# The start addresses of matmul operands in a decoder layer on one core, laid out anew

## The chip, the cores and the metric

The kernel runs on one core of one Trainium2 chip. The metric is the device time of one execution in microseconds. Three runs of the kernel before took 2182.17, 2182.19 and 2182.4 us, median 2182.19.

## The reference

One decoder layer in float32 for 512 tokens of width 2048. What is computed:

```python
hn = rms_norm(x, norm_mix_pre)
q, k, v, gate_b, gate_c, hc = split(hn @ w_in)          # 2048 -> 6 x 1024
a = rms_norm(diff_attention(q, k, v, lam, rel_bias), subln_gain) * (1 - lambda_init)
c = rms_norm(gate_b * short_conv(gate_c * hc, conv_w), conv_norm_gain)
x = x + rms_norm(concat(a, c) @ w_out, norm_mix_post)
hn = rms_norm(x, norm_ffn_pre)
f = (silu(hn @ w_gate) * (hn @ w_up)) @ w_down          # 2048 -> 5632 -> 2048
x = x + rms_norm(f, norm_ffn_post)
```

`diff_attention` has 8 heads; each is the difference of two causal softmaxes (64 wide) with a relative-position bias, times v (128 wide).

## The kernel before

Every large product is done in three passes of a faster 32-bit matmul type (fp32r). An operand is split into a high part, rounded to that type by ScalarE (`split`, L99), and a low part, the rest, by VectorE (L100). `mm3` (L121 to L124) then issues three matmuls for one block of 128 rows of the contraction: high x high (L122), high x low (L123), low x high (L124). In its argument list the first pair, `lhi, llo`, is the stationary operand (128x128, loaded as weights), the second, `rhi, rlo`, the moving one, streamed in 256 or 512 columns. In the profile PE is the matmul, PEld the load of its weights; while one matmul streams, the weights of the next are loaded.

The stages, in order of time:

1. v, first half of its columns, while x is normalised and transposed into `act_hi` and `act_lo` (4 token tiles x 16 blocks x 128, so 32 KB per partition each). Moving: chunks of w_in; stationary: act.
2. v, second half; then 20 column projections (`job_cols`: q, k, h, c, b, four times). Here act moves, 512 columns at a time, and w_in is stationary. Attention for two heads at a time is stepped between them as side work; so are its small matmuls, with tiles of their own (q, k, klo, v, whi, wlo).
3. The output projection (`job_out`, `out_last`). Moving: w_out; stationary: act, which now holds attention and convolution.
4. The norm before the feed-forward part, its transposes (`to_x`) and the sums of quadrants of x that a Strassen scheme needs (`t1` to `t4`).
5. Gate and up (`gate_up`). Each 256 columns of w_gate or w_up are a quartet of blocks, 44 in all, worked in 7 products instead of 8 (`product`). A product is 8 x `mm3` = 24 matmuls of 256 moving columns; the moving operand comes from act or from one of the pairs x0/x1, x2/x3, x4/x5 (`moving`), and `w` is stationary, both parts in one ring tile (high part first, low part 4 KB behind). Product 6 moves x0/x1, product 7 x2/x3, product 4 x4/x5, the others act. Products run in the order 1, 2, 5, 7, 6, 3, 4, but the first four matmuls of product 5 stand ahead of product 2, which waits for ScalarE to copy product 1 out of the bank that it shares.
6. Down (`job_down`, `down_last`): 44 blocks of the hidden activations in 5 groups of 4, 12, 12, 12 and 4. Moving: w_down, 512 columns; stationary: the hidden activations, in group 0 in spare and m3, in groups 1 and 3 in act, in groups 2 and 4 in x0 to x5.

Weights come in chunks of 8 KB per partition into `raw`, are split by ScalarE and VectorE, and the parts go round a ring of four tiles of 8 KB (`ring_tile`): a chunk of w_in, w_out or w_down takes two of them (so the pairs 0, 1 and 2, 3 alternate), a `w` of gate and up takes one. In stage 1 and in the last parts of stages 3 and 6 some chunks go to tiles of another pool (`part` in stage 1, `two_parts` into x tiles later).

Where an operand begins in its partition is set by the pools. In the kernel before, `offset_tile` (L75) asks for a tile of 8 KB + 128 bytes (32 KB + 128 for act) that starts at a multiple of 128 bytes, and uses it from 32 bytes on; a `w` in the ring is used from 96 bytes on (L798, `ring_tile(16, P, ..., 24)`, offsets being in words of 4 bytes). Later tiles lie behind earlier ones, so successive tiles move on by 128 bytes or more. The feed-forward tiles x0 to x5, spare and m3 are made the same way in `place`. Within a tile every block that a matmul reads begins a multiple of 512 bytes from the start of the operand.

Of the kernel before, what the change touches and what calls it, by code (L numbers as in the profile page):

```python
# [12 lines left out]
F32R = mybir.dt.float32r  # L13
# [5 lines left out]
P = 128  # L19
D = 2048  # L20
S = 512
NT = S // P
KC = D // P
# [30 lines left out]
def trunk(ctx: ExitStack, tc: tile.TileContext, a, out):  # L54
    nc = tc.nc
    w_in, w_out, w_gate, w_up, w_down = (a[n][0] for n in ("w_in", "w_out", "w_gate", "w_up", "w_down"))
    x = a["x"][0]
# [8 lines left out]
    def mm_bank(name):  # L66
        return ps.tile([P, 512], F32, tag="mm", name=name)
# [4 lines left out]

    high = ctx.enter_context(tc.tile_pool(name="high", bufs=1, side="right"))

    def offset_tile(pool, words, n, m, tag, name, offset=8, **kw):  # L75

        t = pool.tile([P, words + 32], F32R, tag=tag, name=name, align_bytes=128, **kw)
        return t[:, offset : offset + n * m].rearrange("p (n m) -> p n m", m=m)

    act_hi, act_lo = (  # L80
        offset_tile(high, NT * KC * P, NT * KC, P, n, n).rearrange("p (t k) n -> p t k n", k=KC)
        for n in ("act_hi", "act_lo")
    )
    ring = [0]

    def ring_tile(n, m, name, offset=8):

        i = ring[0] = (ring[0] + 1) % 4
        return offset_tile(high, 2048, n, m, f"ring{i}", name, offset)

    ident = const.tile([P, P], F32, name="ident")
    make_identity(nc, ident)
# [5 lines left out]
    def split(hi, lo, src):  # L98
        nc.scalar.copy(hi, src)  # L99
        nc.vector.tensor_tensor(out=lo, in0=src, in1=hi.bitcast(F32), op=ALU.subtract)  # L100
# [20 lines left out]
    def mm3(o, lhi, llo, rhi, rlo, start, stop):  # L121
        nc.tensor.matmul(o, lhsT=lhi, rhs=rhi, start=start, stop=False)  # L122
        nc.tensor.matmul(o, lhsT=lhi, rhs=rlo, start=False, stop=False)  # L123
        nc.tensor.matmul(o, lhsT=llo, rhs=rhi, start=False, stop=stop)  # L124
# [14 lines left out]
    def scale_rows(xn, xt, r, gB, k4):  # L139
        cs = slice(k4 * 512, (k4 + 1) * 512)  # L140
        nc.vector.scalar_tensor_tensor(
            out=xn[:, cs], in0=xt[:, cs], scalar=r, in1=gB[:, cs], op0=ALU.mult, op1=ALU.mult
        )
# [34 lines left out]
    with start as sp:  # L178
        xts, vch, early = [], [], []
        gB = sp.tile([P, D], F32, tag="gain", name="g_norm_mix_pre")  # L180

        def load_x(t):
            xt = sp.tile([P, D], F32, tag="x", bufs=NT, name=f"x_{t}")
            for c in range(2 if t == 0 else 1):
                cs = slice(c * 1024, (c + 1) * 1024) if t == 0 else slice(0, D)
                nc.sync.dma_start(xt[:, cs], x[t * P : (t + 1) * P, cs])
            xts.append(xt)

        def load_gain(c):
            cs = slice(c * 1024, (c + 1) * 1024)  # L190
            nc.sync.dma_start(gB[:, cs], a["norm_mix_pre"][0:1, cs].broadcast_to([P, 1024]))

        def part(n):
            def parts(name):
                return tuple(offset_tile(sp, 2048, 4, 512, f"{x_}{n}", f"{x_}_{name}") for x_ in ("hi", "lo"))

            return parts

        def v_spec(cg, q4):
            c0 = 2 * A + cg * 512  # L200
            return w_in[q4 * 512 : (q4 + 1) * 512, c0 : c0 + 512], 4, 512, f"v{cg}_{q4}"

        vb = [mm_bank(f"pv_0_{t}") for t in range(NT)]

        def v_part(t, q4):
            for k in range(4):
                kc = 4 * q4 + k
                mm3(vb[t], act_hi[:, t, kc, :], act_lo[:, t, kc, :], vch[q4][0][:, k, :], vch[q4][1][:, k, :], kc == 0, kc == KC - 1)

        def first_norm(t):  # L210
            xn = sp.tile([P, D], F32, tag="xn", bufs=2, name=f"xn_{t}")
            ss = small.tile([P, 2], F32, tag="ss2", name=f"ss_{t}")
            for c in range(2):
                cs = slice(c * 1024, (c + 1) * 1024)
                nc.scalar.activation(xn[:, cs], xts[t][:, cs], AF.Square, accum_out=ss[:, c : c + 1])
            nc.vector.tensor_add(ss[:, 0:1], ss[:, 0:1], ss[:, 1:2])
            r = rsqrt_mean(ss[:, 0:1], 1, D, EPS, f"pre{t}")
            for k4 in range(4):
                scale_rows(xn, xts[t], r, gB, k4)
                to_act(t, xn, k4, f"pre{t}")  # L220

        def v_load(q4):
            vch.append(load_chunk(*v_spec(0, q4), part(q4) if q4 >= 2 else None))

        def bias_rows():

            oh = sp.tile([NB, VL], F32, tag="oh", name="oh")
            nc.sync.dma_start(oh, a["bucket_rows"])
            rb = sp.tile([NB, NH], F32, tag="rb", name="rb")
            nc.sync.dma_start(rb, a["rel_bias"])  # L230
            vec = sp.tile([NH, VL], F32, tag="vec", name="vec")
            for i in range(2):
                b = aux_bank(f"pvec_{i}")
                nc.tensor.matmul(b[:NH, : VL // 2], lhsT=rb, rhs=oh[:, i * (VL // 2) : (i + 1) * (VL // 2)], start=True, stop=True)
                nc.vector.tensor_copy(vec[:, i * (VL // 2) : (i + 1) * (VL // 2)], b[:NH, : VL // 2])
            d1 = dram.tile([NH, VL], F32, name="d1")
            nc.scalar.dma_start(d1, vec)
            d2 = dram.tile([P, NH, VL], F32, name="d2")
            nc.scalar.dma_start(d2, bass.AP(d1.tensor, d1.offset, [[0, P], [VL, NH], [1, VL]]))
            return d2  # L240

        load_x(0)
        load_gain(0)
        load_gain(1)
        first_norm(0)
        v_load(0)
        v_part(0, 0)
        v_load(1)
        load_x(1)
        v_part(0, 1)  # L250
        first_norm(1)
        v_load(2)
        v_load(3)
        load_x(2)
        load_x(3)
        for q4 in range(2):
            v_part(1, q4)
        for q4 in range(2, 4):
            for t in range(2):
                v_part(t, q4)  # L260
        for t in range(2, NT):
            first_norm(t)
            if t == 2:
                d2 = bias_rows()
            for q4 in range(4):
                v_part(t, q4)
                if t == NT - 1 and q4 < 2:
                    early.append(load_chunk(*v_spec(1, q4)))
# [294 lines left out]
    late = {}  # L563
# [5 lines left out]
    def place(tag, dtype=F32, shape=(P, D)):  # L569
        count = late["count"] = late.get("count", 0) + 1  # L570
        name = f"{tag}_{count}"
        if tag[0] == "x" or tag in ("spare", "m3"):
            t = late["fp"].tile([P, D + 32], dtype, tag=tag, bufs=1, name=name, align_bytes=128)
            t = t[:, 8 : 8 + D]
            return t.rearrange("p (n m) -> p n m", m=shape[-1]) if len(shape) == 3 else t
        return late["fp"].tile(list(shape), dtype, tag=tag, bufs=1, name=name)

    def open_ffn(_):
# [24 lines left out]
        return late["mix"][t][:, half * 1024 : (half + 1) * 1024]  # L603

    def act_half(t, half):
        return tuple(x_[:, t, 8 * half : 8 * half + 8, :].rearrange("p k n -> p (k n)") for x_ in (act_hi, act_lo))

    def t_half(n, tau):
        if n not in late:
# [19 lines left out]
    def to_x(t, k4):  # L629

        xn = late["mix"][t][:, k4 * 512 : (k4 + 1) * 512]
        b = aux_bank(f"px_{t}_{k4}")
        for i in range(4):
            nc.tensor.transpose(b[:, i * P : (i + 1) * P], xn[:, i * P : (i + 1) * P], ident)
        nc.scalar.copy(xn, b)
        if t < 2 or k4 >= 2:
            sl = slice(4 * k4, 4 * k4 + 4)
            split(*(x_[:, t, sl, :].rearrange("p k n -> p (k n)") for x_ in (act_hi, act_lo)), b)

    def residual_in(t):  # L640
        late["x", t] = place(f"x{4 + t % 2}")
# [146 lines left out]
    def prepare(n):  # L788

        q, i = order[n]  # L790
        if i in (1, 2) and 0 < q < HEAD:
            src = heads_raw[q][:, 8 * (i - 1) : 8 * i, :]
        else:
            (p11, p21), (p12, p22) = ((r[:, :, :P], r[:, :, P:]) for r in raws[q])
            src = {1: p11, 2: p12, 3: p12, 4: p22, 5: tmp.get("s1"), 6: p21, 7: p21}[i]
            if i in (3, 6):
                combine(q, {3: 4, 6: 2}[i])
        w = ring_tile(16, P, f"w_{q}_{i}", 24).rearrange("p (a k) m -> p a k m", a=2)  # L798
        split(w[:, 0], w[:, 1], src)
        operands[n] = w  # L800

    def moving(i, part, k):
        x_ = (act_hi, act_lo)[part]
        if i in (1, 2):
            return x_[:, 0:2, 8 * (i - 1) + k, :]
        if i in (3, 5):
            return x_[:, 2:4, (8 if i == 3 else 0) + k, :]
        return late[{6: 2, 7: 3, 4: 4}[i]][part].rearrange("p (t k n) -> p t k n", t=2, n=P)[:, :, k, :]
# [215 lines left out]
```

## Time and profile before

| | |
|---|---|
| median of three runs | 2182.19 us |
| the profiled execution | 2182.11 us |
| its span, first to last instruction | 2180.3 us |
| granted TensorE clock, mean | 0.997 |
| PE, PEld busy | 99%, 88% |
| DVE, ACT busy | 60%, 37% |
| chain that ended last | PE 96%, DVE 3%, DMA 1% |
| HBM traffic | 120 GB/s over the span |
| first matmul of gate and up, last one | 792.6 us, 1684.5 us |

A matmul's recorded duration (280 ns at 256 columns, about 390 at 512) overlaps the next matmul's, since matmuls are pipelined: a busy PE says little. What counts is how far apart two matmuls begin, which the timeline gives to 0.01 us, and how many begin in a stretch, which the windows give. PEld is a row of its own: 99% of it in gate and up means that the loads follow each other without a gap.

### The profile page before, as it was taken

What the parts mean: (1) busy time and instruction counts of PE and PEld (TensorE: products, weight loads), DVE (VectorE), ACT (ScalarE), POOL (GpSimd) and SP (SyncE); (2) the same over time, 40 slices, a digit from 0 to 9 for tenths busy, and PEclk for the clock granted to TensorE, in tenths of its full rate; (3) what the DMA queues carried; (4) which work ended last, traced back from release to release, by engine and by line L of the source; (5) the groups of instructions that cost most, each with busy time, mean ns of one, the idle gap of its engine ahead of it and who ended that gap; (6) DMA issues with size and microseconds to landing.
All of it is one profiled execution on the core that took longest, in us unless ns stands there. A gap on an engine that the chain in (4) does not pass through costs nothing.

```text
span 2180.3 us, 30431 instructions
## 1 busy us (share of the span) xinstructions
PE 2149.8 (99%) x13118; PEld 1914.0 (88%) x13118; DVE 1312.7 (60%) x1635; ACT 809.0 (37%) x1065; POOL 30.1 (1%) x51
## 2 busy tenths in 40 slices
PE   7999999999999998999999999999999999999998
PEld 6788888888888888999999999999999888888886
DVE  5226355453642489888888887887887532432336
ACT  4234243433532364444444444444444321211122
POOL 0000000000000000000000000000000000000000
PEclk9999999999999999999999999999999999999999
DMA  7322223222243353343343333333423632423233
GB/s 242 110 97 87 97 86 99 88 85 90 78 177 113 136 174 117 116 136 98 116 136 121 103 126 126 116 108 126 136 95 122 219 135 97 155 97 116 96 115 117
DMA packets 197831, 261.74 MB, mean 120 GB/s; under 512 B 9368, under 2 KB 146584, under 8 KB 195264
## 3 DMA queue, kind: packets, MB, share of 16 engines
q1 hardware_dynamic: 196384, 255.05, 34.7%
q10 hardware_dynamic: 1312, 4.74, 0.7%
q8 instruction: 103, 1.69, 0.3%
q14 instruction: 32, 0.26, 0.0%
HBM read 240.88 MB, written 21.52 MB: 120 GB/s over the span
## 4 chain that ended last, share of the span: by engine, by line
PE 96%; DVE 3%; DMA 1%; issue 0%; ACT 0%; POOL 0%; SPq 0%; DVEq 0%; POOLq 0%; ACTq 0%
PE pd L124 9%; PE pd L123 9%; PE pd L122 9%; PE pa L122 4%; PE pc L124 4%; PE pc L123 4%; PE pc L122 4%; PE pb L122 4%; PE pb L124 4%; PE pb L123 4%; PE pa L124 3%; PE pa L123 3%; PE po L124 3%; PE po L122 3%; PE po L123 3%; PE pv L123 1%
## 5 line engine op out<-in xcount | busy, mean ns | idle before, releaser
L100 DVE TENSOR_TENSOR lo_d<-raw_d,hi_d 128x2048 fp32r<-128x2048 f32 x42 | 96.2, 2291 | 188.1 <-ACT hi_d L99 188.1
L122 PE MATMUL pa<-act_hi,w 128*128 128x256 f32 x704 | 201.7, 286 | 0.7 <-ACT w L99 0.7
L124 PE MATMUL pa<-act_hi,w 128*128 128x256 f32 x704 | 198.3, 282 | 0.3 <-DVE w L100 0.3
L123 PE MATMUL pa<-act_lo,w 128*128 128x256 f32 x704 | 196.9, 280 | 0.0
L99 ACT CAST w<-raw_q 128x1024 fp32r<-128x1024 f32 x130 | 136.5, 1051 | 139.4 <-PE pc L124 39.4
L99 ACT CAST hi_d<-raw_d 128x2048 fp32r<-128x2048 f32 x42 | 80.3, 1913 | 283.1 <-PE pd L124 266.1
L100 DVE TENSOR_TENSOR w<-raw_q,w 128x1024 fp32r<-128x1024 f32 x130 | 156.7, 1221 | 13.7 <-ACT w L99 13.7
L124 PE MATMUL pd<-hi_d,act_lo 128*128 128x512 f32 x384 | 151.4, 394 | 0.0
L122 PE MATMUL pd<-hi_d,act_hi 128*128 128x512 f32 x384 | 150.9, 393 | 0.0
L123 PE MATMUL pd<-lo_d,act_hi 128*128 128x512 f32 x384 | 150.3, 392 | 0.0
L122 PEld LDWEIGHTS pa<-act_hi,w 128*128 128x128 f32 x704 | 132.2, 188 | 8.9 <-ACT m L833 7.9
L124 PEld LDWEIGHTS pa<-act_hi,w 128*128 128x128 f32 x704 | 132.5, 188 | 0.5 <-DVE w L100 0.5
L123 PEld LDWEIGHTS pa<-act_lo,w 128*128 128x128 f32 x704 | 132.7, 188 | 0.0
L124 PE MATMUL pb<-act_hi,w 128*128 128x256 f32 x352 | 98.8, 281 | 3.0 <-DVE w L100 3.0
L122 PE MATMUL pd<-x,w 128*128 128x256 f32 x352 | 99.0, 281 | 1.7 <-ACT w L99 1.7
L124 PE MATMUL pd<-x,w 128*128 128x256 f32 x352 | 99.2, 282 | 1.3 <-DVE w L100 1.3
L124 PE MATMUL pc<-act_hi,w 128*128 128x256 f32 x352 | 98.6, 280 | 0.3 <-DVE w L100 0.3
L123 PE MATMUL pd<-x,w 128*128 128x256 f32 x352 | 98.8, 281 | 0.0
L122 PE MATMUL pb<-x,w 128*128 128x256 f32 x352 | 98.7, 281 | 0.0
L123 PE MATMUL pc<-act_lo,w 128*128 128x256 f32 x352 | 98.7, 280 | 0.0
L123 PE MATMUL pb<-x,w 128*128 128x256 f32 x352 | 98.7, 280 | 0.0
L124 PE MATMUL pb<-x,w 128*128 128x256 f32 x352 | 98.7, 280 | 0.0
(283 smaller groups left out, 6140.3 us busy)
## 6 DMA issues: line engine op xcount, KB each, us to landing
raw_q<-in_w_gate SPq DMA_DIRECT2D x44, 1024.0 KB, 5.1
raw_d<-in_w_down SPq DMA_DIRECT2D x44, 1024.0 KB, 5.0
post<-in_w_up SPq DMA_DIRECT2D x22, 1024.0 KB, 5.1
pre<-in_w_up SPq DMA_DIRECT2D x22, 1024.0 KB, 5.1
raw_o<-in_w_out SPq DMA_DIRECT2D x16, 1024.0 KB, 5.0
hd<-m SPq DMA_DIRECT2D x20, 512.0 KB, 2.8
raw_h<-hd SPq DMA_DIRECT2D x10, 1024.0 KB, 5.3
raw_v<-in_w_in SPq DMA_DIRECT2D x8, 1024.0 KB, 5.8
```

The lines of the kernel that those rows point to most:

```text
L99: nc.scalar.copy(hi, src)
L100: nc.vector.tensor_tensor(out=lo, in0=src, in1=hi.bitcast(F32), op=ALU.subtract)
L122: nc.tensor.matmul(o, lhsT=lhi, rhs=rhi, start=start, stop=False)
L123: nc.tensor.matmul(o, lhsT=lhi, rhs=rlo, start=False, stop=False)
L124: nc.tensor.matmul(o, lhsT=llo, rhs=rhi, start=False, stop=stop)
```

## The change

The padded tiles go. `acts` is one tile that holds act high and low for the projections at words 16 and 8336, and for gate and up at words 0 and 8320, which is 64 bytes lower; these `ffn_hi` and `ffn_lo` overlay the others, and gate and up, with the steps that fill them, now use them. Ring tiles, the start stage's tiles, x0 to x5, spare and m3 are plain tiles of 8 KB. The number, the order, the sizes and the waits of all instructions on all engines are the same in both built programs.

The start of each operand within 512 bytes, from the tile addresses in the two built programs:

| operand | before | after |
|---|---|---|
| act_hi, act_lo in stages 1 to 3, and in down | 288, 416 | 480, 480 |
| act in gate and up (after: ffn_hi, ffn_lo) | 288, 416 | 416, 416 |
| ring tiles 0, 1, 2, 3 with w_in, w_out, w_down | 160, 416, 160, 288 | 480, all four |
| ring tiles 0, 1, 2, 3 with `w` of gate and up | 224, 480, 224, 352 | 480, all four |
| x0, x1, x2, x3, x4, x5 | 160, 416, 160, 416, 32, 288 | 416, all six |
| spare, m3 | 32, 32 | 416, 416 |
| stage 1's own hi and lo tiles (two chunks) | 32, 160 and 416, 160 | 416, all four |
| attention: q, k, klo, v | 416 | 416 |
| attention: whi, wlo, token tiles 0 and 2; 1 and 3 | 416; 480 | 416; 480 |

Whole addresses, in bytes of the partition: before, act_hi begins at 129824, act_lo at 162720, the ring tiles at 195744, 204192, 212640 and 220960; after, act_hi at 130528, act_lo at 163808, the ring at 196576, 204768, 212960 and 221152, 8192 apart.

```diff
-    def offset_tile(pool, words, n, m, tag, name, offset=8, **kw):
-
-        t = pool.tile([P, words + 32], F32R, tag=tag, name=name, align_bytes=128, **kw)
-        return t[:, offset : offset + n * m].rearrange("p (n m) -> p n m", m=m)
-
-    act_hi, act_lo = (
-        offset_tile(high, NT * KC * P, NT * KC, P, n, n).rearrange("p (t k) n -> p t k n", k=KC)
-        for n in ("act_hi", "act_lo")
-    )
+    acts = high.tile([P, 2 * NT * KC * P + 144], F32R, name="acts")
+    act_hi, act_lo, ffn_hi, ffn_lo = (
+        acts[:, o : o + NT * KC * P].rearrange("p (t k n) -> p t k n", k=KC, n=P)
+        for o in (16, 144 + NT * KC * P, 0, 128 + NT * KC * P)
+    )
...
-    def ring_tile(n, m, name, offset=8):
+    def ring_tile(n, m, name):
...
-        return offset_tile(high, 2048, n, m, f"ring{i}", name, offset)
+        return high.tile([P, n, m], F32R, tag=f"ring{i}", name=name)
...
-                return tuple(offset_tile(sp, 2048, 4, 512, f"{x_}{n}", f"{x_}_{name}") for x_ in ("hi", "lo"))
+                return (
+                    sp.tile([P, 4, 512], F32R, tag=f"hi{n}", name=f"hi_{name}"),
+                    sp.tile([P, 4, 512], F32R, tag=f"lo{n}", name=f"lo_{name}"),
+                )
...
-        if tag[0] == "x" or tag in ("spare", "m3"):
-            t = late["fp"].tile([P, D + 32], dtype, tag=tag, bufs=1, name=name, align_bytes=128)
-            t = t[:, 8 : 8 + D]
-            return t.rearrange("p (n m) -> p n m", m=shape[-1]) if len(shape) == 3 else t
         return late["fp"].tile(list(shape), dtype, tag=tag, bufs=1, name=name)
...
-        return tuple(x_[:, t, 8 * half : 8 * half + 8, :].rearrange("p k n -> p (k n)") for x_ in (act_hi, act_lo))
+        return tuple(x_[:, t, 8 * half : 8 * half + 8, :].rearrange("p k n -> p (k n)") for x_ in (ffn_hi, ffn_lo))
...
-            split(*(x_[:, t, sl, :].rearrange("p k n -> p (k n)") for x_ in (act_hi, act_lo)), b)
+            split(*(x_[:, t, sl, :].rearrange("p k n -> p (k n)") for x_ in (ffn_hi, ffn_lo)), b)
...
-        w = ring_tile(16, P, f"w_{q}_{i}", 24).rearrange("p (a k) m -> p a k m", a=2)
+        w = ring_tile(16, P, f"w_{q}_{i}").rearrange("p (a k) m -> p a k m", a=2)
...
-        x_ = (act_hi, act_lo)[part]
+        x_ = (ffn_hi, ffn_lo)[part]
```

## The prediction

> **What bounds the kernel now.** I read the page's busy times and its chain first, then windows of the long stages, then the timeline of single matmuls.
>
> ```profile
> span 2180.3 us, 30431 instructions
> PE 2149.8 (99%) x13118; PEld 1914.0 (88%) x13118; DVE 1312.7 (60%) x1635; ACT 809.0 (37%) x1065; POOL 30.1 (1%) x51
> ...
> PE 96%; DVE 3%; DMA 1%; issue 0%; ACT 0%; POOL 0%; SPq 0%; DVEq 0%; POOLq 0%; ACTq 0%
> ...
> 1000.00:1200.00 200.00, 200.00 (x1682) 198.03 (x1681) 163.18 (x175) 86.96 (x95) 0.00 (x0) 1.00 0.36 119
> 1200.00:1400.00 200.00, 200.00 (x1683) 198.03 (x1682) 163.11 (x175) 87.06 (x96) 0.00 (x0) 1.00 0.36 119
> 1400.00:1600.00 200.00, 200.00 (x1682) 198.03 (x1681) 163.12 (x175) 86.95 (x96) 0.00 (x0) 1.00 0.36 119
> 1728.88:1861.99 133.11, 133.11 (x577) 108.11 (x576) 44.85 (x31) 29.01 (x16) 0.00 (x0) 1.00 0.38 134
> ```
>
> The last four rows are windows; their columns are PE, PEld, DVE, ACT, POOL busy, then clock, DMA share and GB/s. The chain of work is TensorE for 96%, at a granted clock of 1.00, so the time is a count of matmuls times their spacing. I call the time from one matmul's start to the next one's start its pitch. In gate and up 5047 matmuls of 256 columns take 600 us: 118.9 ns each, and there the weight loads (PEld) are busy 99% of the time. In the second down group 577 matmuls of 512 columns take 133.1 us: 230.7 ns each, with PEld busy 81%. So a matmul of 256 columns waits for its weights as much as for its data, and one of 512 columns has room for the load. DVE (82% in gate and up) and DMA (36%) are below their limits.
>
> No instruction, size or wait differs in the changed kernel; only addresses do. The question is what a pitch owes to addresses. While one matmul streams its moving operand, the weights of the next one are loaded. I call D the start of that moving operand minus the start of those weights, in bytes, modulo 512. The table of tile starts ahead of this gives D for every pair. Four chains of 512 columns, each by its first and last start (48, 48, 48 and 4 matmuls):
>
> ```profile
> 1795.44 0.39 PE L122 MATMUL pd<-hi_d,act_hi 128*128 128x512 f32 x1
> ...
> 1806.40 0.40 PE L124 MATMUL pd<-hi_d,act_lo 128*128 128x512 f32 x1
> 1806.64 0.39 PE L122 MATMUL pd<-hi_d,act_hi 128*128 128x512 f32 x1
> ...
> 1817.40 0.39 PE L124 MATMUL pd<-hi_d,act_lo 128*128 128x512 f32 x1
> ...
> 1906.03 0.39 PE L122 MATMUL pd<-hi_d,x 128*128 128x512 f32 x1
> ...
> 1916.68 0.40 PE L124 MATMUL pd<-hi_d,x 128*128 128x512 f32 x1
> ...
> 183.73 0.40 PE L415 MATMUL pss<-k,q 128*128 128x512 f32 x1
> ...
> 184.42 0.39 PE L416 MATMUL pss<-klo,q 128*128 128x512 f32 x1
> ```
>
> The first chain (ring tiles 0 and 1 against act; D 384, 0, 384 over the three matmuls of `mm3`) has a pitch of 10.96/47 = 233.2 ns; the second, same code on ring tiles 2 and 3 (D 384, 384, 384), 10.76/47 = 228.9. The third (ring tiles 0 and 1 against x2 and x3: D 0, 0, 0) has 10.65/47 = 226.6. The fourth, attention scores, has D 0 and all its tiles alike modulo 512, as the change makes nearly every operand; its three pitches are 230 on average, right after other phases. So address alone is worth 6.6 ns of 233, and D = 0 is the lowest.
>
> Now 256 columns: product 6 of quartets 20, 21 and 22 (24 matmuls each), then attention values of an even and an odd head (8 each), and a shorter one (4):
>
> ```profile
> 1216.03 0.28 PE L122 MATMUL pd<-x,w 128*128 128x256 f32 x1
> ...
> 1218.64 0.28 PE L124 MATMUL pd<-x,w 128*128 128x256 f32 x1
> ...
> 1235.95 0.28 PE L122 MATMUL pd<-x,w 128*128 128x256 f32 x1
> ...
> 1238.66 0.28 PE L124 MATMUL pd<-x,w 128*128 128x256 f32 x1
> ...
> 1255.96 0.28 PE L122 MATMUL pd<-x,w 128*128 128x256 f32 x1
> ...
> 1258.67 0.28 PE L124 MATMUL pd<-x,w 128*128 128x256 f32 x1
> ...
> 198.41 0.28 PE L416 MATMUL pss<-klo,q 128*128 128x256 f32 x1
> 198.53 0.28 PE L458 MATMUL pa<-v,whi 128*128 128x256 f32 x1
> ...
> 199.36 0.28 PE L458 MATMUL pa<-v,wlo 128*128 128x256 f32 x1
> 225.88 0.39 PE L124 MATMUL pc_b<-act_hi,lo_b 128*128 128x512 f32 x1
> 226.11 0.28 PE L458 MATMUL pa<-v,whi 128*128 128x256 f32 x1
> ...
> 226.90 0.28 PE L458 MATMUL pa<-v,wlo 128*128 128x256 f32 x1
> 184.66 0.28 PE L458 MATMUL pa<-v,whi 128*128 128x256 f32 x1
> ...
> 185.01 0.28 PE L458 MATMUL pa<-v,wlo 128*128 128x256 f32 x1
> ```
>
> Quartet 20 (w in ring tile 0; D 448, 192, 448) runs at 2.61/23 = 113.5 ns. Quartet 21 (ring tile 3; D 320, 64, 320) runs at 2.71/23 = 117.8, and quartet 22, whose ring tile 2 gives the same D as ring tile 0, at 117.8 too. The two heads have D 448 throughout, the value that the change gives all of gate and up: the even head runs at 0.83/7 = 118.6, the odd one at 0.79/7 = 112.9. So there are two steady pitches, about 117.7 and 113.4, and the address does not settle alone which one a chain takes. What came before does: the odd head follows a matmul of 512 columns, with its weights long loaded; the even head follows 256-column scores at the upper pitch, and stays there. The 118.9 of gate and up says that nearly all its products are at the upper one.
>
> **The change part by part.** The sum is made against the profiled execution, 2182.11 us (span 2180.3 and 1.8 around it), which is the median of 2182.19 within 0.1.
>
> *Gate and up* (44 quartets x 7 products x 24 = 7392 matmuls). Moving operands begin 64 bytes below the weights, so D is 448 everywhere, and it no longer jumps by 128 or 256 bytes between high and low parts or between products. Part of the 118.9 is a stall in each quartet:
>
> ```profile
> 987.52 0.28 PE L122 MATMUL pb<-act_hi,w 128*128 128x256 f32 x1
> 987.79 0.38 PE L122 MATMUL pa<-act_hi,w 128*128 128x256 f32 x1
> 988.01 0.28 PE L123 MATMUL pa<-act_lo,w 128*128 128x256 f32 x1
> ...
> L122 PEld LDWEIGHTS pa<-act_hi,w 128*128 128x128 f32 x704 | 132.2, 188 | 8.9 <-ACT m L833 7.9
> ```
>
> Pitches of 270 and 220 instead of twice 117.7: 255 ns per 168 matmuls, 1.5 ns each, so the undisturbed pitch is 117.4. It is not removed. At the lower pitch the gain is 4.0 x 7392 = 29.6 us. Against it: after a stall the pitch has to settle again (the short chain above: three pitches in 0.35 us, 12 ns over 3 x 113.4), and the four matmuls that cover ACT's copy get 4 ns shorter each: 28 ns x 44 = 1.2 us. Net 28.4. Bounds: nothing (the upper pitch stays), and 113.4 without either loss, 29.6. I take the lower pitch because gate and up is entered from 512-column matmuls of the output projection, as the odd head is, every stall gives the load the same head start, and nothing afterwards shifts D. DVE then works 16.3 us of a quartet of 19.3 us (84%), so its splits still keep ahead.
>
> *512 columns, D = 0.* This holds for 1152 matmuls of down (groups 1 and 3, against act), about 670 of the output projection, 290 of v, all 1920 of the column projections and 96 of the last down group. Down alternates 233.2 and 228.9, mean 231.1; the output projection and v use the same ring pairs against act, so I price them alike. The column projections go by this chain (q and k of the first pair, 192 matmuls):
>
> ```profile
> 115.56 0.39 PE L122 MATMUL pc_q<-act_hi,hi_q 128*128 128x512 f32 x1
> ...
> 159.29 0.39 PE L124 MATMUL pc_k<-act_hi,lo_k 128*128 128x512 f32 x1
> ```
>
> 43.73/191 = 229.0. At 226.6: down, output, v and the rest 2208 x 4.5 = 9.9 us; columns 1920 x 2.4 = 4.6, less some 50 interruptions by attention that each cost three or four pitches of 230 instead of 226.6 (0.7 us). Together 13.8. Bounds: nothing, if they stay at the 230 of the scores (columns 2 us longer, the rest 2 us shorter), and 14.5.
>
> *512 columns, D = 64 or 448.* In 864 matmuls of down (groups 0, 2 and half of the last) the weights lie in x, spare or m3, 64 bytes below the ring; in some 190 of v and output it is the other way round. No chain of 512 columns here has either. Bounds from the chains above, 226.6 and 233.2 around today's mean of about 229.5: a gain of 3 us or a loss of 4. I take 0, the middle.
>
> *ACT, DVE, DMA.* Same work into other addresses. TensorE's 99% covers them; only the head and the norm between the output projection and gate would show a change, and an instruction there would have to get much slower to matter.
>
> Sum: 28.4 + 13.8 = 42.2 us; 2182.1 - 42.2 = 2140 us.
>
> [...]
>
> **The rivals.**
> *Gate and up keep the upper pitch*, as quartet 22 does with the same D as quartet 20: for it speaks that 117.7 is the common state, against it that D then jumped at each product and now does not. 2182 - 13.8 = 2168. Or they take it by turns, ring tile by ring tile: half of the 28.4, 2154.
> *Nothing moves*: the sum over an `mm3` triple is fixed by something else, and other chains pay what these save. 2182. Against it stand whole chains of 48 and 24 that differ.
> *Slower*: with all tiles alike, load and stream run in step and meet at the same place in every matmul, where now only some do. The nearest row is the first pitch of the short chain, 184.66 to 184.78, 122 ns; a chain held there costs 4.6 x 7392 = 34 us, and 512 columns held at 233.2 cost some 10 us more: 2226. It decides if gate and up stay above 119.3, where the gain of 13.8 is used up. Against it: the same chain leaves 122 within three matmuls, and no long chain shows more than 118 or 233.
>
> ```profile
> 184.78 0.28 PE L458 MATMUL pa<-v,wlo 128*128 128x256 f32 x1
> ```
>
> **How the numbers follow.** Lower pitch everywhere, 2140: 0.62, by itself 2134 to 2149. By turns, 2154: 0.10. Upper pitch in gate and up, 2168: 0.13. No change: 0.07. Slower: 0.08. The range 2133 to 2169 leaves out the last two cases. A measurement of this kernel can tell 0.2% (4.4 us) from no change: faster 0.85, same 0.07, slower 0.08.
>
> **What would show it.** In gate and up some 1743 matmuls per 200 us (168 in 19.3 us) instead of 1682; still 1682 means the upper pitch. In down, groups 1 and 3: every chain of 48 at 226.6, no more alternation. Group 2 tells what D = 64 costs. PEld and DVE shares in gate and up rise, the idle time before L122 stays near 8 us. The prediction is wrong if chains of D = 0 run at 230 or above, or if gate and up split by ring tile.

## The result, and the profile after

The changed kernel takes 2143.78 us (median of four runs, 2143.53 to 2144.97) against 2182.25 for the kernel before in the same series: a ratio of 0.9825, 95% interval 0.9808 to 0.9842. That is 38.5 us less; the forecast was 42.2 less, 2140. The profiled execution took 2143.53 us. The page of the changed kernel:

```profile
span 2141.7 us, 30431 instructions
PE 2110.2 (99%) x13118; PEld 1886.7 (88%) x13118; DVE 1308.1 (61%) x1635; ACT 809.3 (38%) x1065; POOL 30.2 (1%) x51
...
PE 94%; DVE 4%; DMA 1%; issue 0%; ACT 0%; POOL 0%; SPq 0%; DVEq 0%; POOLq 0%; ACTq 0%
...
L119 PEld LDWEIGHTS pa<-acts,w 128*128 128x128 f32 x704 | 132.2, 188 | 9.2 <-ACT m L829 8.2
```

The shares hardly move: TensorE is still busy 99% of the span and still carries the chain. The same 13118 matmuls simply begin closer together. The stall behind ACT's copy in each quartet is still there (8.2 us in all, 7.9 before). Windows of gate and up: first its first four quartets, then the other 40, of the kernel after and of the kernel before, and three stretches of 200 us after.

```profile
785.23:877.62 92.39, 84.01 (x690) 82.15 (x688) 89.62 (x101) 50.82 (x65) 2.79 (x2) 0.96 0.47 149
877.62:1651.60 773.98, 773.66 (x6722) 765.80 (x6721) 645.54 (x697) 351.46 (x380) 0.00 (x0) 1.00 0.36 122
1000.00:1200.00 200.00, 199.93 (x1735) 197.96 (x1734) 167.70 (x182) 90.54 (x99) 0.00 (x0) 1.00 0.38 127
1200.00:1400.00 200.00, 199.92 (x1742) 197.95 (x1741) 166.53 (x181) 90.16 (x98) 0.00 (x0) 1.00 0.37 125
1400.00:1600.00 200.00, 199.91 (x1739) 197.75 (x1738) 168.66 (x183) 91.03 (x99) 0.00 (x0) 1.00 0.36 119
```

```profile
792.59:884.38 91.79, 83.99 (x689) 82.25 (x688) 89.52 (x101) 50.85 (x65) 2.79 (x2) 0.98 0.48 150
884.38:1684.50 800.12, 800.12 (x6722) 792.22 (x6721) 649.78 (x697) 350.11 (x380) 0.00 (x0) 1.00 0.35 118
```

Forty quartets went from 800.1 to 774.0 us (the windows above), and 1735 to 1742 matmuls begin in 200 us where 1682 did (forecast 1743). The first four quartets did not gain: 91.8 before, 92.4 after.

Single chains, by their first and last starts in the timeline: product 6 of quartet 22, a chain of down group 1 (weights in act, D 0), a chain of group 2 (weights in x, D 64).

```profile
1237.50 0.28 PE L119 MATMUL pd<-x,w 128*128 128x256 f32 x1
...
1240.11 0.28 PE L121 MATMUL pd<-x,w 128*128 128x256 f32 x1
...
1706.51 0.39 PE L119 MATMUL pd<-hi_d,acts 128*128 128x512 f32 x1
...
1717.16 0.39 PE L121 MATMUL pd<-hi_d,acts 128*128 128x512 f32 x1
...
1837.18 0.39 PE L119 MATMUL pd<-hi_d,x 128*128 128x512 f32 x1
...
1847.94 0.39 PE L121 MATMUL pd<-hi_d,x 128*128 128x512 f32 x1
```

The product runs at 2.61/23 = 113.5 ns (113.3 on average over the stage), where it ran at 117.8 before. The chain of group 1 runs at 10.65/47 = 226.6, and the chains of groups 1 and 3 average 226.7, without the alternation of 233.2 and 228.9. The chain of group 2 runs at 10.76/47 = 228.9.

The time by stage, between starts of matmuls in the two traces (us):

| stretch | before | after | change | forecast |
|---|---|---|---|---|
| start to the first column projection (v) | 115.6 | 113.8 | -1.8 | -1.3 |
| column projections, with attention between | 491.4 | 488.6 | -2.9 | -3.9 |
| output projection | 185.6 | 182.9 | -2.7 | -3.0 |
| gate and up, first 4 quartets | 91.8 | 92.4 | +0.6 | -2.6 |
| gate and up, 40 quartets | 800.2 | 774.0 | -26.2 | -25.8 |
| down, groups 0 to 3 | 442.4 | 436.9 | -5.5 | -5.2 |
| down, last group | 43.9 | 43.7 | -0.2 | -0.4 |

(The forecast's terms are split by matmuls: 28.4 over 44 quartets; 4.5 ns for each of 290, 670, 1152 and 96 matmuls.) The changes sum to 38.7. Of the 3.5 us that are missing, 3.2 belong to four quartets.

### The profile page after: what moved, and what is told of

It reads as the page before. It is cut to its first block, busy times and chain, and to the rows that moved or that the text cites. A ratio compares the mean times of both kernels' runs of the same rounds, so it can differ in the third digit from the quotient of the medians.

```text
span 2141.7 us, 30431 instructions
## 1 busy us (share of the span) xinstructions
PE 2110.2 (99%) x13118; PEld 1886.7 (88%) x13118; DVE 1308.1 (61%) x1635; ACT 809.3 (38%) x1065; POOL 30.2 (1%) x51
## 4 chain that ended last, share of the span: by engine, by line
PE 94%; DVE 4%; DMA 1%; issue 0%; ACT 0%; POOL 0%; SPq 0%; DVEq 0%; POOLq 0%; ACTq 0%
PE pd L121 9%; PE pd L120 9%; PE pd L119 9%; PE pa L119 4%; PE pc L121 3%; PE pc L119 3%; PE pc L120 3%; PE pb L121 3%; PE pb L119 3%; PE pb L120 3%; PE pa L120 3%; PE pa L121 3%; PE po L119 3%; PE po L120 3%; PE po L121 3%; PE pc_h L119 1%
## 5 line engine op out<-in xcount | busy, mean ns | idle before, releaser
L119 PE MATMUL pa<-acts,w 128*128 128x256 f32 x704 | 199.1, 283 | 1.1 <-ACT w L96 0.8
L121 PE MATMUL pa<-acts,w 128*128 128x256 f32 x704 | 194.8, 277 | 0.3 <-DVE w L97 0.3
L120 PE MATMUL pa<-acts,w 128*128 128x256 f32 x704 | 195.0, 277 | 0.0
L119 PE MATMUL pd<-hi_d,acts 128*128 128x512 f32 x384 | 149.4, 389 | 0.0
L121 PE MATMUL pd<-hi_d,acts 128*128 128x512 f32 x384 | 149.4, 389 | 0.0
L120 PE MATMUL pd<-lo_d,acts 128*128 128x512 f32 x384 | 149.4, 389 | 0.0
L119 PEld LDWEIGHTS pa<-acts,w 128*128 128x128 f32 x704 | 132.2, 188 | 9.2 <-ACT m L829 8.2
L121 PEld LDWEIGHTS pa<-acts,w 128*128 128x128 f32 x704 | 132.2, 188 | 0.5 <-DVE w L97 0.5
L120 PEld LDWEIGHTS pa<-acts,w 128*128 128x128 f32 x704 | 132.2, 188 | 0.0
L121 PE MATMUL pb<-acts,w 128*128 128x256 f32 x352 | 98.1, 279 | 3.0 <-DVE w L97 3.0
L119 PE MATMUL pb<-acts,w 128*128 128x256 f32 x352 | 97.9, 278 | 0.1
L121 PE MATMUL pc<-acts,w 128*128 128x256 f32 x352 | 97.3, 276 | 0.5 <-DVE w L97 0.5
L120 PE MATMUL pb<-acts,w 128*128 128x256 f32 x352 | 97.8, 278 | 0.0
L119 PE MATMUL pc<-acts,w 128*128 128x256 f32 x352 | 97.2, 276 | 0.0
L120 PE MATMUL pc<-acts,w 128*128 128x256 f32 x352 | 97.2, 276 | 0.0
```

## The experiments

In all of them the instructions of every engine stand in the order of the changed kernel, except where an operand's tile has another name; only addresses differ. Theory A is the prediction's: the pitch is set by D. What the runs had to tell: whether it is a difference of starts at all, of which two starts, modulo what, and whether its value or its constancy counts.

### The 64 bytes taken away

```diff
-    acts = high.tile([P, 2 * NT * KC * P + 144], F32R, name="acts")
+    acts = high.tile([P, 2 * NT * KC * P + 128], F32R, name="acts")
...
-        for o in (16, 144 + NT * KC * P, 0, 128 + NT * KC * P)
+        for o in (0, 128 + NT * KC * P, 0, 128 + NT * KC * P)
...
+        late["fp"].tile([P, 16], F32, tag="pad", name="pad")
```

> Gate's and up's moving operands (act copies and x0 to x5) begin at the same byte of 512 as the weights: D = 0 in all of gate and up and, through x0 to x5, in down groups 0, 2 and 4. Theory A (the value of D decides): 512 columns at D 0 run at 226.7 ns, so groups 0 and 2 go from 228.9 to 226.7 (863 matmuls, 1.9 us less), but 256 columns leave the lower pitch; at 117.7 instead of 113.3 ns that is 40 quartets x 0.65 us = 26 us more: 2168 us. Theory B (only that D stays constant matters): gate and up stay at 113.3 ns, 2142 us. Theory C (whole addresses matter, the 64 bytes don't): 2144 us, and groups 0 and 2 stay at 228.9 ns.

Measured: 2184.55 us, ratio to before 1.001 (1.0 to 1.0019). The whole gain is gone. A window of gate and up, and product 6 of quartet 20:

```profile
1000.00:1200.00 200.00, 200.00 (x1650) 198.10 (x1649) 161.47 (x174) 85.41 (x94) 0.00 (x0) 1.00 0.36 118
```

```profile
1216.67 0.28 PE L119 MATMUL pd<-x,w 128*128 128x256 f32 x1
...
1219.43 0.28 PE L121 MATMUL pd<-x,w 128*128 128x256 f32 x1
```

2.76/23 = 120.0 ns, and so in every product of the 40 quartets, where the kernel before had 117.7: a third steady pitch that no trace had shown, above both that the prediction knew. The 40 quartets take 815.8 us, 41.7 more than after. At the same time groups 0 and 2 of down go to 226.7 ns, as expected of D 0. So D 0 is the lowest of the values tried at 512 columns and the highest at 256. Theories B and C fall; A has its direction but not its size (26 us expected).

### 256 bytes instead of 64

```diff
-        for o in (16, 144 + NT * KC * P, 0, 128 + NT * KC * P)
+        for o in (64, 192 + NT * KC * P, 0, 128 + NT * KC * P)
```

(with `acts` 48 words longer and x0 to x5 moved along)

> Gate's and up's moving operands begin 256 bytes below the weights (D 256 throughout gate and up, 256 in down groups 0, 2 and 4). Theory A (the value of D decides): no row shows a chain of constant D 256; between 113.3 and 117.7 ns, most likely the upper, 2144 + 26 = 2170 us. Theory B (that D is constant is enough): 113.3 ns, 2144 us. Down groups 0 and 2 between 226.7 and 233.2 ns, 2 us less to 4 us more.

Measured: 2184.61 us, ratio 1.0011 (1.0001 to 1.002).

```profile
1000.00:1200.00 200.00, 200.00 (x1649) 198.10 (x1648) 161.40 (x173) 85.03 (x94) 0.00 (x0) 1.00 0.36 118
```

Again 120.0 ns in all of the 40 quartets, and 226.7 ns in groups 0 and 2 of down. D 256 is the same as D 0 on both sides. Expected was 2170: constancy is not enough, and a pitch above 117.7 was not foreseen.

### Everything 160 bytes lower

```diff
+            late["top"] = high.tile([P, 40], F32, name="top")
...
+        late["fp"].tile([P, 88], F32, tag="pad", name="pad")
```

(`top` lies above the ring and pushes ring and act down; the second pad moves x0 to x5, spare and m3 by as much, modulo 512)

> All operands of the projections, of gate and up and of down lie 160 bytes lower than in the changed kernel; every D between them is the same. Theory A (only the difference D counts): 2144 us, every stage's pitch the same. Theory C (the place of the operand within 512 bytes or the whole address counts): pitches return towards those of before, 117.7 in gate and up and 229 to 233 elsewhere, up to 2182 us.

Measured: 2142.16 us (2141.83 to 2142.89), ratio 0.9816 (0.98 to 0.9833).

```profile
1000.00:1200.00 200.00, 199.92 (x1741) 197.95 (x1740) 167.78 (x181) 90.71 (x99) 0.00 (x0) 1.00 0.38 127
```

113.3 ns in gate and up, 226.7 and 228.9 in down as after. So in these stages a shift of all operands by 160 bytes changes no pitch; what counts is the distance between them. (Stage 1's own tiles did not move along, so some 90 matmuls of v have another D than in the changed kernel.) The 1.6 us less come from the first four quartets (91.6 instead of 92.4 us), from the columns (488.0 instead of 488.6) and from a quartet that after lies at the upper pitch and here does not.

### Ring tiles that are not whole multiples of 8 KB apart

```diff
-        return high.tile([P, n, m], F32R, tag=f"ring{i}", name=name)
+        t = high.tile([P, n * m + (0, 128, 128, 128)[i]], F32R, tag=f"ring{i}", name=name)
+        return t[:, steps[i] : steps[i] + n * m].rearrange("p (n m) -> p n m", m=m)
```

(`steps` is 0 for all four)

> The ring tiles begin 8704 bytes apart instead of 8192, and act_hi and act_lo lie 1536 bytes lower; every D modulo 512 is that of the changed kernel, none of the ring's distances is a multiple of 8 KB. Theory A (D modulo 512 or a part of it counts): 2143.8 us, 113.3 and 226.7 ns as there. Theory C (multiples of 8 KB count): 2150 to 2182 us.

Measured: 2144.62 us, ratio 0.9823 (0.981 to 0.9837): the changed kernel's time, with its pitches (1741 matmuls begin between 1000 and 1200 us). What counts is the start modulo 512 or a part of it, not the 8 KB.

### Gate and up alone

```diff
-        for o in (16, 144 + NT * KC * P, 0, 128 + NT * KC * P)
+        for o in (48, 208 + NT * KC * P, 0, 128 + NT * KC * P)
...
+        t = high.tile([P, n * m + (0, 128, 0, 128)[i]], F32R, tag=f"ring{i}", name=name)
+        return t[:, steps[i] : steps[i] + n * m].rearrange("p (n m) -> p n m", m=m)
```

(`steps` is 0, 64, 0, 32 words for chunks, and 0 for `w`)

> Gate and up as in the changed kernel (D 448 throughout), but the ring tiles as used by w_in, w_out and w_down, and act_hi and act_lo, begin at the bytes of 512 relative to each other that the kernel before had (D 384, 0, 384 and 384, 384, 384 in the chains). Theory A (D decides, the stages are independent): gate and up at 113.3 ns, groups 1 and 3 of down at 233.2 and 228.9 by turns as before; 2182.2 - 25.5 = 2157 us, 2 us more or less for groups 0 and 2, whose D is neither kernel's. Rival (how gate and up are entered decides: they take the lower pitch only behind an output projection that runs at 226.7): gate and up at 117.7 ns, 2182 us.

Measured: 2159.64 us, ratio 0.9898 (0.9883 to 0.9913).

```profile
1000.00:1200.00 200.00, 199.91 (x1741) 197.94 (x1740) 166.85 (x181) 89.78 (x98) 0.00 (x0) 1.00 0.38 124
```

Gate and up run at 113.3 ns behind an output projection that averages 232 ns, so the rival falls: the lower pitch does not come from how the stage is entered. The 40 quartets take 773.5 us. The steps were laid one ring tile off, so the other stages do not have the kernel before's D but 0, 256, 0 and 128, 256, 128 over the three matmuls, and their chains in groups 1 and 3 run at 231.4 and 233.1 instead of 233.2 and 228.9. That is an experiment of its own: constant 0 and constant 256 both give 226.7, but by turns, with moving operands that start 128 bytes apart by turns too, they give 231.4. In the profiled execution (2162.99 us, the longest of four) the 40 quartets are 26.7 us shorter than before, but down is 2.0 longer, the columns 1.8, the output projection 0.6 and the first four quartets, which wait for their operands, 3.9. The 2157 that were expected left these out.

### D stepped from ring tile to ring tile

```diff
-        return high.tile([P, n, m], F32R, tag=f"ring{i}", name=name)
+        t = high.tile([P, n * m + (0, 128, 128, 128)[i]], F32R, tag=f"ring{i}", name=name)
+        return t[:, steps[i] : steps[i] + n * m].rearrange("p (n m) -> p n m", m=m)
```

(`steps` is 0, 32, 64, 96 words for `w`, 0 for the rest)

> As the changed kernel, but the weights of gate and up lie 0, 128, 256 and 384 bytes higher in ring tiles 0 to 3: D is constant within a product of 24 matmuls, 448, 320, 192 and 64 in turn. Theory A with a period of 256 bytes (D 256 gave the pitches of D 0): products at 192 like those at 448, 113.3 ns; products at 320 and 64 alike, between 113.3 and 120.0. Theory A with a period of 512: 113.3 at 448 alone. Rival (a jump of D between products upsets the pitch whatever its value): 117.7 ns in all products.

Measured: 2144.56 us, ratio 0.9824 (0.9806 to 0.9842). Products 6, 3 and 4 of quartet 20 and product 1 of quartet 21, at D 320, 192, 64 and 448:

```profile
1199.55 0.28 PE L120 MATMUL pd<-x,w 128*128 128x256 f32 x1
...
1202.16 0.28 PE L122 MATMUL pd<-x,w 128*128 128x256 f32 x1
1202.27 0.28 PE L120 MATMUL pc<-acts,w 128*128 128x256 f32 x1
...
1204.88 0.28 PE L122 MATMUL pc<-acts,w 128*128 128x256 f32 x1
1204.99 0.28 PE L120 MATMUL pc<-x,w 128*128 128x256 f32 x1
...
1207.60 0.28 PE L122 MATMUL pc<-x,w 128*128 128x256 f32 x1
1207.71 0.28 PE L120 MATMUL pa<-acts,w 128*128 128x256 f32 x1
...
1210.32 0.28 PE L122 MATMUL pa<-acts,w 128*128 128x256 f32 x1
```

2.61/23 = 113.5 each. All four values are as good as 448, and a jump of the weights by 128 bytes between products costs nothing. These are also the four values that gate and up had in the kernel before, at 117.7. So what held the kernel before at 117.7 was not the value of D.

### Finer steps

```diff
-        w = ring_tile(16, P, f"w_{q}_{i}", (0, 32, 64, 96)).rearrange("p (a k) m -> p a k m", a=2)
+        w = ring_tile(16, P, f"w_{q}_{i}", (0, 8, 16, 104)).rearrange("p (a k) m -> p a k m", a=2)
```

(the difference to the run above; steps in words, chunks keep 0)

> As before, with the weights of gate and up 0, 32, 64 and 416 bytes higher in ring tiles 0 to 3: D 448, 416, 384 and 32 in turn, constant within a product. Theory A with a period of 256: 384 is 128 from both slow values (0 and 256 gave 120.0 ns), so it is at the lower pitch, 113.3; 416 lies between two values at the lower pitch and is there too; 32 is near 0 and lies between 113.3 and 120.0. Theory A with 448 as a single good value: 113.3 ns in a quarter of the products alone.

Measured: 2170.38 us, ratio 0.9942 (0.9924 to 0.996). Product 1 of quartet 20, at D 416:

```profile
1198.42 0.28 PE L120 MATMUL pa<-acts,w 128*128 128x256 f32 x1
...
1201.18 0.28 PE L122 MATMUL pa<-acts,w 128*128 128x256 f32 x1
```

2.76/23 = 120.0. Averaged over the 40 quartets without their stalls, D 416 has 119.4, 384 has 118.5, 32 has 117.0 and 448 has 114.9 (each with the settling behind its neighbour). Both numbers expected for 384 and 416 are wrong: a period of 128 fits, one of 256 does not. At 256 columns D = 64 modulo 128 is good and D = 0 or 32 modulo 128 is not. The three new values are rough: 416 and 32 are alike modulo 128 and yet differ by 2.4 ns, and each always follows the same other value.

### The low part of act moved

```diff
-        for o in (16, 144 + NT * KC * P, 0, 128 + NT * KC * P)
+        for o in (16, 144 + NT * KC * P, 0, 32 + NT * KC * P)
```

> As the changed kernel, but ffn_lo lies 128 bytes higher modulo 512 against ffn_hi: products 1, 2, 5 and 3 have D 448 and 64 by turns over the high and low passes (both are good values by themselves: 113.3 ns each when constant within a product); products 7, 6 and 4, from x tiles, keep 448. Theory A (the value of D modulo 128 alone decides): 113.3 ns in all products, 2144 us. Theory D (value and constancy within a product): products 1, 2, 5, 3 at 117.7 ns, 96 x 4.4 ns x 40 = 17 us more, 2161 us; 2169 us if the others stay at 117.7 behind them.

Measured: 2164.61 us, ratio 0.9917 (0.9888 to 0.9946).

```profile
1000.00:1200.00 200.00, 200.00 (x1699) 197.84 (x1698) 164.39 (x178) 88.18 (x97) 0.00 (x0) 1.00 0.36 119
```

The products from act, with D 448, 64, 448, average 117.7 ns; those from x stay at 113.3 in most quartets, and in some at 117.7 behind them, which puts the time between the 2161 and the 2169 that were expected. Two good values by turns, with a moving operand that starts 128 bytes apart by turns, are a bad pair. This is the pitch of the kernel before, made again with one edit.

### The low parts of act and of the weights moved together

```diff
-        w = ring_tile(16, P, f"w_{q}_{i}").rearrange("p (a k) m -> p a k m", a=2)
-        split(w[:, 0], w[:, 1], src)
+        t = ring_tile(16, P, f"w_{q}_{i}")
+        w = tuple(t[:, o : o + 1024].rearrange("p (k m) -> p k m", k=8) for o in (0, 1056))
+        split(*w, src)
```

(on top of the edit above; the ring tiles are longer and the x tiles moved so that D is 448 elsewhere)

> As the run before, and the low part of each w lies 128 bytes higher too. Now D is constant, 448, in products 1, 2, 5 and 3, while their moving operand starts at two bytes of 512 by turns; in products 7, 6 and 4 the moving operand always starts at the same byte and D is 448, 320, 448. Theory D (difference to the next weights counts): products 1, 2, 5, 3 at 113.3 ns, products 7, 6, 4 at 117.7: 72 x 4.4 ns x 40 = 13 us more, 2157 us. Rival (the moving operand's own start has to stay the same from matmul to matmul): the other way round, 2161 us. Rival (any tile that differs from the rest): all at 117.7, 2169 us.

Measured: 2170.76 us, ratio 0.9942 (0.992 to 0.9965). Products 1 and 6 of quartet 20:

```profile
1197.48 0.28 PE L120 MATMUL pa<-acts,w 128*128 128x256 f32 x1
...
1200.23 0.29 PE L122 MATMUL pa<-acts,w 128*128 128x256 f32 x1
...
1209.09 0.28 PE L120 MATMUL pd<-x,w 128*128 128x256 f32 x1
...
1211.70 0.28 PE L122 MATMUL pd<-x,w 128*128 128x256 f32 x1
```

Product 1, whose D is 448 in every matmul but whose moving operand starts 128 bytes apart by turns, has 2.75/23 = 119.6 ns, with single pitches up to 130. Product 6, whose D goes 448, 320, 448 but whose moving operand always starts at the same byte, has 2.61/23 = 113.5. So it is the rival's way round: at jumps of 128 bytes, what has to stay the same is the moving operand's own start from matmul to matmul. (The time is above the rival's 2161 because the pitch is 120, not 117.7.)

### D 0 in every 512-column chain, 448 in gate and up

```diff
+        up = 16 if len(shape) == 3 and tag != "m3" else 0
+        if tag in ("x0", "x1", "x2", "x3"):
+            if "xs" not in late:
+                late["xs"] = late["fp"].tile([P, 4 * D + 128], F32R, name="xs")
+            o = int(tag[1]) * D + up
+            t = late["xs"][:, o : o + D]
+        elif tag in ("x4", "x5"):
+            t = late["fp"].tile([P, D + (128 if tag == "x4" else 16)], dtype, tag=tag, bufs=1, name=name)[:, up : up + D]
+        elif tag == "m3":
+            t = late["fp"].tile([P, D + 128], dtype, tag=tag, bufs=1, name=name)[:, 16 : 16 + D]
...
```

(and a pad of 16 words ahead of stage 1's tiles)

> Gate and up as in the changed kernel (D 448); every 512-column operand at D 0: x0 to x5 are used 64 bytes higher in down and in the output projection than in gate and up, spare, m3 and stage 1's own chunks lie 64 bytes higher. Theory A: down groups 0, 2 and 4 go from 228.9 to 226.7 ns (863 matmuls, 1.9 us), the output projection's 92 matmuls at D 448 from 233.3 to 226.7 (0.6 us), as many of v (0.6 us, if TensorE sets the time there): 2143.8 - 3.1 = 2140.7 us, between 2140 and 2142 as quartets come to lie at the upper pitch. Rival (those chains are held by something else): 2143.8 us.

Measured: 2140.31 us (2139.83 to 2140.92), ratio 0.9804 (0.979 to 0.9817). A chain of group 2:

```profile
1857.95 0.39 PE L119 MATMUL pd<-hi_d,xs 128*128 128x512 f32 x1
...
1868.60 0.39 PE L121 MATMUL pd<-hi_d,xs 128*128 128x512 f32 x1
```

10.65/47 = 226.6 where it was 228.9. Because the difference to the changed kernel is small, the two were run again on one chip:

> The changed kernel beside the run that follows, on one chip: 2143.8 us, 0.75 us more for each quartet that lies at 117.7 ns.

> D 0 in every 512-column chain, 448 in gate and up, on the same chip as the changed kernel. Theory A: 1.7 us less in down, 0.4 us in its last group, 0.6 us each in v and the output projection: 3.3 us below the changed kernel in the same call, 2140.5 us. Rival (the difference between the two calls was the chip's): the same time as the changed kernel.

Measured: 2143.6 us (2143.47 to 2144.6) and 2140.75 (2140.48 to 2141.27), with ratios to before of 0.9824 (0.9811 to 0.9837) and 0.9809 (0.9796 to 0.9823). The two sets of runs do not overlap: 2.85 us of the 3.3 expected. In the two traces groups 0 to 3 of down take 436.9 and 435.2 us, the last group 43.7 and 43.3, the output projection 182.9 and 182.4. The 0.6 us that were expected of v did not come: it takes 113.9 and 114.0 us. This version beats both kernels.

## Why the prediction was right, and where it was not

**Gate and up at the lower pitch: right, for a reason only half right.** The steady pitch is 113.3, and 40 quartets gained 26.2 us where 25.8 were counted. The stated reason was that D "no longer jumps". The runs put two conditions in its place. The moving operand's start must not go to and fro by 128 bytes from matmul to matmul: 117.7 in the run with act's low part moved, and about 120 with act and weights moved together, though D there never jumps. And of the values tried D must be 64 modulo 128 (all four such values give 113.5 in the single products above): 120.0 at 0 and 256. The kernel before met the second in all its products and broke the first in those from act; the change meets both. My D mixed the two, since within a product of the kernel before every jump of D came with a jump of the moving operand's start.

Two things stay open here. In the kernel before, the products from x move parts that begin 256 bytes apart, not 128. Most of them ran at 118 ns as well, but product 6 did so in 30 of the 40 quartets only: in ten, every fourth one, quartet 20 among them, it ran at 113.5 with the same jumps. No run tests 256 bytes alone. And I take D against the weights of the next matmul; in every run with a constant moving start the weights of a product begin alike modulo 128, so the runs do not tell the next weights from the matmul's own.

**The term that was too large: 28.4 for 44 quartets.** I priced all 7392 matmuls at 4.0 ns, the first four quartets too. There TensorE waits for its operands. (Where nothing waits, the matmuls do begin closer, 114 ns apart instead of 117.) The timeline of quartet 0, product 5, in the changed kernel, and a window behind the pause:

```profile
812.25 0.28 PE L120 MATMUL pb<-acts,w 128*128 128x256 f32 x1
815.48 0.58 PE L121 MATMUL pb<-acts,w 128*128 128x256 f32 x1 [2.95 <-DVE w L97]
```

```profile
815.50:818.30 2.80, 2.80 (x13) 2.80 (x14) 2.80 (x3) 0.00 (x0) 0.00 (x0) 0.50 0.00 0
```

DVE's split of `w` comes 2.95 us late; TensorE is busy 84.0 of 92.4 us in these quartets, as before (84.0 of 91.8), and DVE 89.6 of 92.4. Faster matmuls mostly reach the next wait sooner. Besides, the granted clock is 0.50 behind this pause for 13 matmuls, 213 ns each, some 1.3 us. In the trace of the kernel before, a pause as long at the same place (819.53 to 822.76) was followed by matmuls at the full clock (1.00 from 822.8 to 825.4). (Both kernels have such a stretch in product 6 of quartet 0: 0.55 from 832.2 to 835.2 before, 0.54 from 826 to 829 after.) All the other traces of this case have the pause too, and behind it a stretch of 12 to 27 matmuls at 213 ns, which begins at once or up to ten matmuls later. What sets off the half clock no run shows. I should have read the windows of these four quartets before I multiplied.

**How the lower pitch is reached: wrong.** I took it because gate and up is entered from 512-column matmuls "as the odd head is". The first two products of quartet 0 run at 117.7 in the changed kernel, straight behind the output projection, and the odd heads, whose tiles kept their addresses, went up. Attention values of the first odd head after:

```profile
223.58 0.28 PE L458 MATMUL pa<-v,whi 128*128 128x256 f32 x1
...
224.40 0.28 PE L458 MATMUL pa<-v,wlo 128*128 128x256 f32 x1
```

0.82/7 = 117, where it was 112.9. With everything 160 bytes lower the odd heads run at 113.2 again, at the same D. So there are indeed two steady states at one address pattern, as quartets 20 and 22 had said, but what enters them is finer than "from 512 columns". Nor does the trace show the "head start" that a stall was to give the load: behind ACT's copy in quartet 20 (below) the load of the first matmul's weights is recorded from 1191.01 us, as that matmul is. That gate and up took the lower pitch all the same is, on the stated reason, luck. What did change for the odd heads is the pair at their entrance, the last matmul of a column projection (moving act high, from 288 before, 480 after, 320 with everything lower) and `whi` at 480: D 320, 0 and 352. In all traces with D 0 there, odd heads run at 117.7 or 117.9; at 320 and 352 they run at 113.1 to 113.9. That pair is a candidate, no more: in the run with gate and up alone even heads went to 113.5 behind an unchanged pair. The stalls show the two states too. Behind ACT's copy in quartet 20 and in quartet 13:

```profile
1190.72 0.28 PE L119 MATMUL pb<-acts,w 128*128 128x256 f32 x1
1191.01 0.38 PE L119 MATMUL pa<-acts,w 128*128 128x256 f32 x1
1191.23 0.29 PE L120 MATMUL pa<-acts,w 128*128 128x256 f32 x1
1191.35 0.28 PE L121 MATMUL pa<-acts,w 128*128 128x256 f32 x1
1191.47 0.28 PE L119 MATMUL pa<-acts,w 128*128 128x256 f32 x1
1191.58 0.28 PE L120 MATMUL pa<-acts,w 128*128 128x256 f32 x1
...
1054.68 0.28 PE L119 MATMUL pb<-acts,w 128*128 128x256 f32 x1
1054.96 0.39 PE L119 MATMUL pa<-acts,w 128*128 128x256 f32 x1
1055.19 0.28 PE L120 MATMUL pa<-acts,w 128*128 128x256 f32 x1
1055.30 0.28 PE L121 MATMUL pa<-acts,w 128*128 128x256 f32 x1
1055.42 0.28 PE L119 MATMUL pa<-acts,w 128*128 128x256 f32 x1
```

The first settles over 220, 120 and 120 to 113.3. The second goes 230, 110, 120 and stays at 117.7 until the next stall, 168 matmuls on, which costs 0.75 us; that is why only 1735 matmuls begin between 1000 and 1200 us. After the fourth quartet, one quartet did so in this execution and none in another one of the same kernel. What decides between the two behind a stall is open; no run tested it.

**The settling behind stalls** was counted at 28 ns a quartet, 1.2 us. Products 2 and 5 together now lie 299 ns above 48 steady pitches, and lay 258 above theirs before: 41 ns, 1.8 us. Small, and right in sign.

**512 columns, D 0: right.** 226.7 ns on average in the chains of down. Down gave 5.5 us of which 5.1 are the 1152 matmuls at D 0, v 1.8 for 1.3 forecast, the output projection 2.7 for 3.0. The columns gave 2.9 for 3.9: q and k, with hardly any attention between, reach 227.0 and 226.7 on average, h, c and b some 228, so the interruptions cost more than the 0.7 us that I allowed. The reason, that D alone sets the pitch, was half right here too. Two chains of 48 of the kernel before have D 128 in every matmul: a column projection (ring tiles 2 and 3 against act, whose parts begin 128 bytes apart) and group 2 of down (ring tiles 0 and 1, 256 bytes apart, against x4 and x5).

```profile
126.56 0.39 PE L122 MATMUL pc_q<-act_hi,hi_q 128*128 128x512 f32 x1
...
137.32 0.39 PE L124 MATMUL pc_q<-act_hi,lo_q 128*128 128x512 f32 x1
...
1883.89 0.39 PE L122 MATMUL pd<-hi_d,x 128*128 128x512 f32 x1
...
1894.81 0.40 PE L124 MATMUL pd<-hi_d,x 128*128 128x512 f32 x1
```

The first has 10.76/47 = 228.9 ns, the second 10.92/47 = 232.3. So a jump of the moving operand's start (or of the weights', which jump by as much here) counts beside D at 512 columns as well; only at D 0 did a jump of 256 bytes cost nothing (226.6 in the prediction's third chain).

**512 columns, D 64 and 448.** The 0 stood for a middle between 3 us gained and 4 lost. D 64 came out at 228.9 ns, 0.5 below the mean before, a gain of 0.4 us over groups 0 and 2; D 448 at 233.3, where v and the output projection use x or stage 1's tiles. The run with D 0 everywhere shows that both ends were real, and that the change left 2.85 us in the 512-column chains.

**The rivals.** "Upper pitch stays" fell with the first window. "By turns, ring tile by ring tile" fell too: the few products at 117.7 follow the time, not the tile. "Nothing moves" does not agree with this case: 113.3, 117.7 and 120.0 ns are pitches of the same instructions, and the starts alone separate 2140.3 from 2184.6 us. The slower rival deserves more credit than its 0.08. A steady state above 117.7 does exist, at 120.0 ns (I had priced 122). It is D 0, and with the tiles aligned and no 64 bytes the time would have been 2184.6, slower than before. The reason given for it, load and stream meeting at the same place in every matmul, was my guess; no run shows it. The prediction called D 0 "the lowest" from 512-column rows; at 256 columns it has the highest pitch of all constant D, and only the change's 64 bytes keep gate and up away from it.

## What to carry to other kernels

Where TensorE is 99% busy, compare the pitch of long chains of equal matmuls before anything else: a spread among identical instructions (113.3, 117.7 and 120.0 ns at 256 columns, 226.7 to 233.3 at 512) was here, for the most part, a matter of where operands start, and the gain was had without moving an instruction. Let the high and low parts of a moving operand start at the same byte of 512 (113.3 ns against 117.7 to 120 at 256 columns here), and choose the distance to the weights by the column count, by trial: here 64 modulo 128 for 256 columns and 0 modulo 256 for 512. A gain per matmul counted here only where matmuls follow each other without a wait (the first four quartets took 91.8 us before and 92.4 after), so read the windows of a stage's first loops apart from the rest.

## What the runs showed of the hardware that was not expected

- At 256 columns, with a constant moving start, the pitch depends on the start of the moving operand minus that of the weights: 113.3 ns at 64, 192, 320 and 448; 120.0 at 0 and 256; 118.5 at 384, 119.4 at 416 and 117.0 at 32 (these three only stepped from product to product).
- At 512 columns, with a moving operand that always starts at the same byte of 512, the order is another: 226.7 at 0 and 256, 228.9 at 64, 233.3 at 448.
- Moving operands that start 128 bytes apart by turns cost 4 to 7 ns per matmul of 256 columns at distances that are good by themselves; weights that do so cost nothing (113.5 ns).
- At 512 columns D 128 in every matmul gave 228.9 ns where both operands jump by 128 bytes and 232.3 where they jump by 256.
- At a good distance there are still two steady states, 113.3 and 117.7 ns; a stall of about 0.3 us can change from one to the other, and they then hold for 168 matmuls.
- Attention's chains changed state in four of eight heads (the odd ones: 113.7 to 113.9 ns before, 117.7 after) although none of their own tiles had moved modulo 512.
- Behind the wait of 2.95 us in quartet 0 the granted clock was 0.50 for 12 to 27 matmuls in 13 of 14 traces, at once or up to ten matmuls later; in the trace of the kernel before it stayed at 1.00.
